# Permuted moving weights in five down-projection chunks of a hybrid decoder layer

## The chip, the cores and the metric

The kernel runs on one core of one Trainium2 chip. The metric is the device time of one execution in microseconds (us), given as the median of the runs. A profile of one execution, taken by the hardware profiler, shows what each engine did: TensorE (PE in the profile, with PEld for its weight loads), VectorE (DVE), ScalarE (ACT), GpSimd (POOL) and SyncE (SP).

## What is computed

One decoder layer on 256 tokens of width 2048, all in float32. The part around the change is the second half of the layer, the MLP, with its residual add and the last norm:

```python
x = x + mixed @ w_out[l]
h = rms_norm(x, norm2_g[l])
x = x + jnp.square(jax.nn.relu(h @ w_mlp_in[l])) @ w_mlp_out[l]
return rms_norm(x, final_norm_g)
```

`w_mlp_in` is 2048 x 8192 and `w_mlp_out` is 8192 x 2048. Ahead of it stand an input projection, a forgetting attention and a dilated attention, which the change does not touch.

## The kernel before

**Two parts for each number.** A float32 product is made of three products of a reduced type (`fp32r`): each operand is split into a high part, rounded to `fp32r`, and a low part, the rest. ACT writes the high part (`whi`) from the loaded weights (`raw`), and DVE subtracts it from the weights to get the low part (`wlo`). TensorE then adds high times high, high times low and low times high into one PSUM bank.

**Chunks and steps.** The weights are cut into chunks of 512 columns. The MLP runs in four rounds r = 0 to 3. In each round four chunks `u` (columns of `w_mlp_in`) give 2048 hidden values, and four chunks `d` (key `(r, c)`, 512 columns c of `w_mlp_out`, 2048 rows r) add them into the output. A chunk has 16 row blocks of 128, and a step is two of them, so that a plain chunk has 8 steps. `split` makes the two parts of one step's weights (128 partitions x 1024 numbers), and `products` multiplies them.

**Plain and seven.** Of the sixteen `d` chunks ten go through seven products in place of eight (`split_seven`, `seven_products`, with sub-steps "near", "first", "odd" and "even"). The other six are plain: (0,3), (1,3), (2,3), (3,0), (3,2) and (3,3). The last of them, (3,3), has code of its own (`last_chunk`). `weave` strings the steps of a plain chunk and of units of seven into one order, by patterns that are written out by hand; chunk (r,3) of the first three rounds, for example, follows `"1 A2 2 A3 2 B0"`: one plain step, then a unit of seven, and so on.

**A plain `d` step on TensorE.** `product` is called with `parts` = 2, so that each row block and each half of the tokens (128 of 256) takes two halves of 256 columns with three products each: 2 row blocks x 2 token halves x 2 column halves x 3 = 24 matmuls. The activations are the stationary operand (`big_hi`, `big_lo`), and the weights are the moving operand, 256 columns at a time, which lie in order in `whi` and `wlo`.

**The split of a plain step** is one ACT instruction and one DVE instruction over the whole step:

```python
nc.scalar.activation(hi[:, :, c:c + step], t[:, :, c:c + step], AF.Copy)
...
nc.vector.tensor_tensor(lo, t, hi.bitcast(F32), op=ALU.subtract)
```

**What sets the order.** Each engine runs its instructions in the order in which the program gives them. Splits are made some steps ahead of the products: as many as tiles are free for `whi` and `wlo` (four from one pool, and a fifth pair, `whi5` and `wlo5`, in the MLP). A split therefore waits until TensorE has finished with an older step's tile. Between the splits stand the side works, which `at` puts behind given steps: `drain_u`, `rest_u`, `mix_activations` and `split_mixed` for the hidden values, `drain_seven` and `drain_d` for the output.

Of the kernel before, what the change touches and what calls it, by code (L numbers as in the profile page):

```python
# [28 lines left out]
CW = 512  # L29
# [46 lines left out]
def kernel(  # L76
# [18 lines left out]
    nc = tc.nc  # L95
# [22 lines left out]
    def take_bank():  # L118

        n = free_banks.pop(0)  # L120
        t = psum.tile([P, CW], F32, name=f"bank{n}")
        number[id(t)] = n
        return t
# [4 lines left out]
    chunks = []  # L128
# [4 lines left out]
    for g, (vc, qc, kc, half, kind) in enumerate(groups):  # L133
        for what, c0 in (("q", qc), ("v", vc), ("k", kc)):
            cols = CW + NH if (g == 0 and what == "v") else CW
# [65 lines left out]
    raws, splits = {}, {}  # L201
# [30 lines left out]
    def drop(ci, unit):  # L232
        free_raws.append(slots.pop((ci, unit)))
# [44 lines left out]
    def split(i, j0=0, n=2):  # L278
# [13 lines left out]
        splits[i] = (hi, lo)  # L292
        split_rows(i, j0, n)

    def split_rows(i, j, n):
        ci, s, _ = steps[i]
        if s % 2 and j + n == 2:
            drop(ci, s // 2)
        hi, lo = (a[:, j:j + n, :] for a in splits[i])
        t = raws[ci, s // 2][:, 2 * (s % 2) + j:2 * (s % 2) + j + n, :chunks[ci][5]]  # L300
        cols = t.shape[2]
        step = cols // 2 if i == j == 0 else cols
        for c in range(0, cols, step):
            nc.scalar.activation(hi[:, :, c:c + step], t[:, :, c:c + step], AF.Copy)  # L304
        nc.vector.tensor_tensor(lo, t, hi.bitcast(F32), op=ALU.subtract)  # L305
# [169 lines left out]
    accs = {}  # L475

    def operands(what, key):
        if what == "o":
            return yT_hi, yT_lo, key[0] * NH
        if what == "d":  # L480
            return *squares(), 0
        return aT_hi, aT_lo, 0

    def product(acc, a, kt, t, w, j, cols, go, end, narrow=False):

        (ah, al, base), (hi, lo) = a, w
        xh, xl = (p[:, base + kt, t * P:(t + 1) * P] for p in (ah, al))
        for n, (x, part) in enumerate(((xh, hi), (xh, lo), (xl, hi)) if narrow else ((xh, hi), (xl, hi), (xh, lo))):
            nc.tensor.matmul(acc, x, part[:, j, cols], start=go and n == 0, stop=end and n == 2,  # L489
                             skip_group_check=True)  # L490

    def turned_product(ci, i, j, kt, kts):


        if kt == 0:
            accs[ci] = [take_bank() for _ in range(2)]
        hi, lo = splits[i]
        terms = ((hi, aT_hi), (hi, aT_lo), (lo, aT_hi))
        order = [(b, n) for b in range(4) for n in range(3)]
        if i == j == 0:  # L500
            order.sort(key=lambda bn: bn[1])
        for b, n in order:
            acc = accs[ci][b // 2][:, b % 2 * SEQ:(b % 2 + 1) * SEQ]
            w, a = terms[n]
            nc.tensor.matmul(acc, w[:, j, b * P:(b + 1) * P], a[:, kt, :],  # L505
                             start=kt == 0 and b % 2 == 0 and n == 0, stop=kt == kts - 1 and n == 2,
                             skip_group_check=True)

    def products(i, j):
        ci, s, sub = steps[i]  # L510
        what, key, _, _, _, cols, kts = chunks[ci]
        if sub:
            return seven_products(i, j)
        kt = 2 * s + j
        if what in TURNED:
            return turned_product(ci, i, j, kt, kts)
        a = operands(what, key)
        if ci in mixed:
            for t in range(TB):
                product(held(ci, t), a, kt, t, splits[i], j, slice(0, CW), first_in(ci, t), i == last_step[ci] and j == 1)  # L520
            return
        if cols > CW:
            return gated_products(ci, i, j, kt, kts, a)
        if kt == 0:
            accs[ci] = [take_bank() for _ in range(TB)]
        go, end = kt == 0, kt == kts - 1
        parts = 2 if what == "d" else 1
        for t in range(TB):
            for c in range(0, CW, CW // parts):
                cols = slice(c, c + CW // parts)  # L530
                product(accs[ci][t][:, cols], a, kt, t, splits[i], j, cols, go and c == 0, end, parts > 1)

    begun_banks = set()

    def held(ci, n):
        four_banks = accs.setdefault(ci, [None] * 4)
        if four_banks[n] is None:
            four_banks[n] = take_bank()
        return four_banks[n]

    def first_in(ci, n):
        fresh = (ci, n) not in begun_banks
        begun_banks.add((ci, n))
        return fresh

    def seven_products(i, j):

        ci, s, sub = steps[i]
        half, k1, k2 = CW // 2, 2 * s + j, 2 * s + 2 + j
        lower, upper = slice(0, P), slice(P, SEQ)  # L550
        if ci in mixed:
            h, m, base = (aT_hi, aT_lo), forms, KT - FIRST
        else:
            h, m, base = squares(), (mix_hi, mix_lo), 0
        todo = {
            "near": ((0, 0, h, k2, lower), (0, half, m, k2 - base, lower)),
            "first": ((2, 0, h, k1, lower),),
            "odd": ((3 if ci in mixed else 1, half, m, k2 - base, upper), (2, half, m, k1 - base, lower)),
            "even": ((3, 0, m, k1 - base, upper), (1, 0, h, k2, upper)),
        }[sub]  # L560
        hi, lo = splits[i]
        for n, (bank, c0, (ah, al), k, tokens) in enumerate(todo):
            acc = held(ci, bank)[:, c0:c0 + half]
            fresh = first_in(ci, bank)
            for x, (a, w) in enumerate(((ah, hi), (ah, lo), (al, hi))):
                nc.tensor.matmul(acc, a[:, k, tokens], w[:, j, n * half:(n + 1) * half], start=fresh and x == 0,  # L566
                                 stop=s == KT // 2 - 2 and j == 1 and x == 2, skip_group_check=True)

    def gated_products(ci, i, j, kt, kts, a):

        if kt == 0:
            accs[ci] = [take_bank() for _ in range(3)]
        half = CW // 2
        for t in range(TB):
            for acc, c0, c1, go in ((accs[ci][0][:, t * half:(t + 1) * half], 0, half, t == 0),
                                    (accs[ci][1 + t][:, :half + NH], half, CW + NH, True)):
                product(acc, a, kt, t, splits[i], j, slice(c0, c1), go and kt == 0, kt == kts - 1)
# [528 lines left out]
    for ci, (what, key, *_rest) in enumerate(chunks[:-1]):  # L1106
        e = last_slot[what, key]
# [11 lines left out]
        elif what in "qk":  # L1119
# [90 lines left out]
    for i in range(final):  # L1210
        if i == mlp_start:
            attention.close()
            late5 = ctx.enter_context(tc.tile_pool(name="late5", bufs=1))
            late5.tile([P, 24], F32R, name="late_begin")
            late = late_forms.enter_context(tc.tile_pool(name="late", bufs=1))
            late_tiles.update(ring=late5, pool=late)
            for n in ("whi5", "wlo5"):
                late5.tile([P, 2 * CW + LINE], F32R, name=n)
            late5.tile([P, 2, CW // 2], F32, name="copies")
            late5.tile([P, 4, CW], F32, name="raw4")  # L1220
            free_raws.append(4)
            late.tile([P, MIX_HI], F32R, name="late_hi")
            mix_hi = late.tile([P, KT, SEQ], F32R, name="mix_hi")
            late.tile([P, MIX_LO], F32R, name="late_lo")
            mix_lo = late.tile([P, KT, SEQ], F32R, name="mix_lo")
            late.tile([P, LINE - (MIX_HI + MIX_LO) % LINE], F32R, name="late_end")
        load_more()
        while free_tiles(i) if i + LEAD < final else done < upto.get(i, i + LEAD):
            done += 1
            split(done)  # L1230
            load_more()
        for j in range(2):
            products(i, j)
            run_side(2 * i + j)
# [31 lines left out]
```

## Time and profile before

| | |
|---|---|
| median of 2 runs | 1072.07 us (1072.02 to 1072.12) |
| profiled execution, its own time | 1072.24 us |
| its span | 1070.5 us |
| mean granted TensorE clock | 0.998 |
| PE busy | 1059.5 us, 8729 matmuls |
| DVE busy | 879.1 us, 1228 instructions |
| ACT busy | 633.4 us, 881 instructions |
| HBM read | 220.09 MB |

The span runs from the first to the last instruction that the profile shows; the execution's own time has 1.74 us more around it. The duration of a matmul in the profile is the time it spends in a pipeline, and several overlap; what one matmul costs in a stream is the distance from start to start, which the chain of work shows (a time divided by a count). For the other engines a mean duration is what an instruction occupies, with little overlap between neighbours.

### The profile page before, as it was taken

The page shows a single profiled execution, that of the slowest core. Times are in us where ns is not written, and L with a number is a line of the kernel's source. Part 1 is how long each engine was busy: PE and PEld are TensorE (multiplying, and loading weights), DVE is VectorE, ACT ScalarE, POOL GpSimd, SP SyncE. Part 2 cuts the span into 40 slices and gives each one's busy share as a digit, 9 for nine tenths or more (in the row PEclk, how much of TensorE's full clock was granted, in tenths as well). Part 3 has the DMA queues.
Part 4 walks back from the last instruction along what each step waited for, and adds up shares of the span by engine and source line. Part 5 has one row for each costly group of instructions (what it writes and reads, how often), then busy time and mean ns, then how long its engine had stood idle before and what let it go on. Part 6 is the DMA issues. An engine that isn't in the chain of part 4 may idle for free.

```text
span 1070.5 us, 21145 instructions
## 1 busy us (share of the span) xinstructions
PE 1059.5 (99%) x8729; PEld 1033.2 (97%) x8729; DVE 879.1 (82%) x1228; ACT 633.4 (59%) x881; POOL 85.2 (8%) x88
## 2 busy tenths in 40 slices
PE   9999999999999999999999999999999999999996
PEld 7999999999988889999999999999999999999996
DVE  6687797887786666678989898988898998897885
ACT  6555556556555565566556666556666656766551
POOL 0011211101001000000100001000000110000000
PEclk9999999999999999999999999999999999999999
DMA  9765565466665567657786677776768776674762
GB/s 322 244 206 189 144 230 162 137 226 179 220 243 173 169 225 216 200 165 217 220 268 173 208 246 237 226 214 196 247 184 257 221 246 215 187 273 146 215 227 80
DMA packets 118189, 223.57 MB, mean 209 GB/s; under 512 B 4723, under 2 KB 17612, under 8 KB 117708
## 3 DMA queue, kind: packets, MB, share of 16 engines
q1 hardware_dynamic: 104684, 208.69, 57.5%
q0 software_dynamic: 12816, 13.12, 8.0%
q8 instruction: 68, 1.11, 0.4%
q10 hardware_dynamic: 592, 0.40, 0.2%
q14 instruction: 29, 0.24, 0.1%
HBM read 220.09 MB, written 2.11 MB: 208 GB/s over the span
## 4 chain that ended last, share of the span: by engine, by line
PE 99%; DMA 0%; DVE 0%; POOL 0%; ACTq 0%; DVEq 0%; issue 0%
PE bank L505 49%; PE bank L489 26%; PE bank L566 21%; PE bank L428 1%; PE bank L880 1%; PE bank L820 1%; PE bank L860 0%; DMA xs<-in_x_dram 0%; PE bank L816 0%; PE bank L882 0%; PE bank L810 0%; PE bank L814 0%; DVE xs L1075 0%; PE bank L884 0%; PE bank L644 0%; POOL rstd L1065 0%
## 5 line engine op out<-in xcount | busy, mean ns | idle before, releaser
L505 PE MATMUL bank<-aT_hi,whi 128*128 128x256 f32 x1536 | 427.1, 278 | 0.0
L505 PE MATMUL bank<-aT_hi,wlo 128*128 128x256 f32 x1536 | 424.4, 277 | 0.0
L505 PE MATMUL bank<-aT_lo,whi 128*128 128x256 f32 x1536 | 424.2, 276 | 0.0
L305 DVE TENSOR_TENSOR wlo<-raw,whi 128x1024 fp32r<-128x1024 f32 (+2 forms) x291 | 349.9, 1215 | 70.7 <-ACT whi L304 68.4
L304 ACT ACTIVATE whi<-raw 128x1024 fp32r<-128x1024 f32 (+2 forms) x292 | 300.6, 1045 | 89.3 <-PE bank L505 39.2
L505 PEld LDWEIGHTS bank<-aT_hi,whi 128*128 128x128 f32 x1536 | 288.2, 188 | 1.1 <-issue 0.9
L505 PEld LDWEIGHTS bank<-aT_lo,whi 128*128 128x128 f32 x1536 | 288.4, 188 | 0.2
L505 PEld LDWEIGHTS bank<-aT_hi,wlo 128*128 128x128 f32 x1536 | 288.3, 188 | 0.1
L267 ACT ACTIVATE whi<-raw 128x1024 fp32r<-128x1024 f32 (+1 forms) x178 | 167.3, 948 | 160.4 <-PE bank L505 55.7
L268 DVE TENSOR_TENSOR wlo<-raw,whi 128x1024 fp32r<-128x1024 f32 (+1 forms) x178 | 194.6, 1095 | 52.6 <-ACT whi L267 50.7
L489 PE MATMUL bank<-whi,big_hi 128*128 128x256 f32 (+1 forms) x488 | 150.3, 308 | 0.0
L489 PE MATMUL bank<-wlo,big_hi 128*128 128x256 f32 (+1 forms) x488 | 149.4, 306 | 0.0
L489 PE MATMUL bank<-whi,big_lo 128*128 128x256 f32 (+1 forms) x488 | 149.3, 306 | 0.0
L489 PEld LDWEIGHTS bank<-wlo,big_hi 128*128 128x128 f32 x488 | 91.6, 188 | 5.1
L489 PEld LDWEIGHTS bank<-whi,big_hi 128*128 128x128 f32 x488 | 91.7, 188 | 4.5
L489 PEld LDWEIGHTS bank<-whi,big_lo 128*128 128x128 f32 x488 | 91.7, 188 | 4.5
L220 POOL DMA_DIRECT2D raw<-in_w_mlp_out_dram x40 | 48.1, 1203 | 559.3 <-DMA raw<-in_w_mlp_out_dram 252.7
L566 PE MATMUL bank<-whi,mix_lo 128*128 128x256 f32 x320 | 88.4, 276 | 0.0
L566 PE MATMUL bank<-whi,mix_hi 128*128 128x256 f32 x320 | 88.4, 276 | 0.0
L566 PE MATMUL bank<-wlo,mix_hi 128*128 128x256 f32 x320 | 88.4, 276 | 0.0
L566 PE MATMUL bank<-whi,big_hi 128*128 128x256 f32 x240 | 66.3, 276 | 0.0
L566 PE MATMUL bank<-whi,big_lo 128*128 128x256 f32 x240 | 66.3, 276 | 0.0
(228 smaller groups left out, 1436.7 us busy)
## 6 DMA issues: line engine op xcount, KB each, us to landing
raw<-in_w_mlp_in_dram SPq DMA_DIRECT2D x64, 1024.0 KB, 6.1
raw<-in_w_mlp_out_dram SPq DMA_DIRECT2D x64, 1024.0 KB, 6.7
raw<-in_w_in_dram SPq DMA_DIRECT2D x42, 1024.0 KB, 5.3
raw<-in_w_out_dram SPq DMA_DIRECT2D x16, 1024.0 KB, 5.1
raw<-in_w_mlp_out_dram POOLq DMA_DIRECT2D x40, 256.0 KB, 4.8
raw<-in_w_in_dram SPq DMA_DIRECT2D x4, 1040.0 KB, 9.6
xs<-in_x_dram SPq DMA_DIRECT2D x1, 2048.0 KB, 10.1
xs<-in_x_dram SPq DMA_DIRECT2D x3, 512.0 KB, 5.7
```

Source lines behind the costliest of these rows:

```text
L220: nc.gpsimd.dma_start(t[:, :2, CW // 2:CW], src[:, :2, :CW // 2], accum_op=ALU.add)
L267: nc.scalar.activation(hi, x, AF.Copy)
L268: nc.vector.tensor_tensor(lo, x, hi.bitcast(F32), op=ALU.subtract)
L304: nc.scalar.activation(hi[:, :, c:c + step], t[:, :, c:c + step], AF.Copy)
L305: nc.vector.tensor_tensor(lo, t, hi.bitcast(F32), op=ALU.subtract)
L428: nc.tensor.transpose(p[:, j * SEQ + t * P:j * SEQ + (t + 1) * P], xs[:, t, c:c + P], ident)
L489: nc.tensor.matmul(acc, x, part[:, j, cols], start=go and n == 0, stop=end and n == 2, skip_group_check=True)
L505: nc.tensor.matmul(acc, w[:, j, b * P:(b + 1) * P], a[:, kt, :], start=kt == 0 and b % 2 == 0 and n == 0, stop=kt == kts - 1 and n == 2, s ...
L566: nc.tensor.matmul(acc, a[:, k, tokens], w[:, j, n * half:(n + 1) * half], start=fresh and x == 0, stop=s == KT // 2 - 2 and j == 1 and x ...
L820: nc.tensor.matmul(s[:, c0:c1], q[:, a, h, rows], k[:, b, h, keys], start=False, stop=n == 2, skip_group_check=True)
L880: nc.tensor.matmul(y[:, :SEQ], v[:, 0, dims], p[:, m, :SEQ], start=n == 0, stop=False, skip_group_check=True)
```

## The change

`split_rows` gets a second way for five of the plain `d` chunks, which a table `walks` names. In this way each step is split in four pieces of 128 x 256 (two row blocks, two column halves) in place of one of 128 x 1024: four ACT and four DVE instructions. Each piece is written into its 256 places in another sequence. `written` views the loaded weights as they are, and `in_order` views the places in the order in which the columns must be read. `product` gives TensorE the view `in_order` of the moving operand, so that the columns come out in their old order. Nothing else moves: the loads, the tiles, the number of matmuls, the order of the steps and the side works stay.

The table has three numbers (a, b, e) for each chunk. The 256 places are b groups of a runs of e neighbours, and column number (i, j, k) of a x b x e lies at place (j, i, k). With e = 4, TensorE reads runs of 4 neighbours (16 bytes) and jumps between them; in places of 4 bytes:

| chunk | (a, b, e) | what TensorE reads one after the other |
|---|---|---|
| (0,3) | (32, 2, 4) | a run of 4, the run 128 places on, back to the next run |
| (1,3) | (2, 32, 4) | runs of 4, 8 places apart, in two passes |
| (2,3) | (4, 16, 4) | runs of 4, 16 places apart, in four passes |
| (3,0) | (2, 128, 1) | single numbers, 2 places apart, in two passes |
| (3,2) | (8, 8, 4) | runs of 4, 32 places apart, in eight passes |

```diff
@@ split_rows
+    walks = {(0, 3): (32, 2, 4), (1, 3): (2, 32, 4), (2, 3): (4, 16, 4), (3, 0): (2, 128, 1), (3, 2): (8, 8, 4)}
+
+    def walk(ci):
+        what, key = chunks[ci][:2]
+        return walks.get(key) if what == "d" else None
+
+    def in_order(x, ci):
+        a, b, e = walk(ci)
+        if b == 2:
+            return x.rearrange("p (b a e) -> p a b e", b=2, e=4)
+        if e == 1:
+            return x.rearrange("p (b a) -> p a b", a=a)
+        return x.rearrange("p (b a e) -> p a b e", a=a, e=e)
+
+    def written(x, ci):
+        a, b, e = walk(ci)
+        if b == 2:
+            return x.rearrange("p (a b e) -> p a b e", b=2, e=4)
+        if e == 1:
+            return x.rearrange("p (a b) -> p a b", a=a)
+        return x.rearrange("p (a b e) -> p a b e", a=a, e=e)
+
     def split_rows(i, j, n):
         ...
+        if walk(ci):
+            for k in range(n):
+                for c in range(0, CW, CW // 2):
+                    cs = slice(c, c + CW // 2)
+                    nc.scalar.activation(in_order(hi[:, k, cs], ci), written(t[:, k, cs], ci), AF.Copy)
+                    nc.vector.tensor_tensor(in_order(lo[:, k, cs], ci), written(t[:, k, cs], ci),
+                                            in_order(hi[:, k, cs], ci).bitcast(F32), op=ALU.subtract)
+            return
@@ product
-            nc.tensor.matmul(acc, x, part[:, j, cols], start=go and n == 0, stop=end and n == 2,
-                             skip_group_check=True)
+            y = part[:, j, cols]
+            nc.tensor.matmul(acc, x, in_order(y, ci) if ci is not None and walk(ci) else y, start=go and n == 0,
+                             stop=end and n == 2, skip_group_check=True)
@@ products
-                product(accs[ci][t][:, cols], a, kt, t, splits[i], j, cols, go and c == 0, end, parts > 1)
+                product(accs[ci][t][:, cols], a, kt, t, splits[i], j, cols, go and c == 0, end, parts > 1, ci)
```

The first place to look at is DVE's queue in chunk (1,3), from the split of its second plain step to that of its fourth. `wlo` is the low part that is written; `nat`, `big_lo` and `mix_lo` belong to the side works on the hidden values. DVE before:

```order
L305 TENSOR_TENSOR wlo<-raw_7422,whi 128x1024 [waits PE_49,Activation_49]
L961 TENSOR_TENSOR big_lo<-nat,big_hi 128x512
L961 TENSOR_TENSOR big_lo<-nat,big_hi 128x512 [waits Activation_49]
L268 TENSOR_TENSOR wlo<-raw_7442,whi 128x2x2x256 [waits Activation_49]
L968 TENSOR_TENSOR nat<-nat 128x2x128 [waits DVE_49]
L969 TENSOR_TENSOR nat<-nat 128x2x128 [waits DVE_49]
L971 TENSOR_TENSOR nat<-nat 128x2x128 [waits DVE_49]
L972 TENSOR_TENSOR nat<-nat 128x2x128 [waits DVE_49]
L305 TENSOR_TENSOR wlo_7794<-raw_7476,whi_7793 128x1024 [waits DMAHW1_49,Activation_49]
L305 TENSOR_TENSOR wlo<-raw_7476,whi 128x1024 [waits Activation_49]
```

The same place on DVE in the changed kernel, where the lines have moved down by the new functions:

```order
L328 TENSOR_TENSOR wlo<-raw_7470,whi 128x2x32x4 [waits PE_49,Activation_49]
L328 TENSOR_TENSOR wlo<-raw_7470,whi 128x2x32x4 [waits Activation_49] x3
L992 TENSOR_TENSOR big_lo<-nat,big_hi 128x512
L992 TENSOR_TENSOR big_lo<-nat,big_hi 128x512 [waits Activation_49]
L268 TENSOR_TENSOR wlo<-raw_7490,whi 128x2x2x256 [waits Activation_49]
L999 TENSOR_TENSOR nat<-nat 128x2x128 [waits DVE_49]
L1000 TENSOR_TENSOR nat<-nat 128x2x128 [waits DVE_49]
L1002 TENSOR_TENSOR nat<-nat 128x2x128 [waits DVE_49]
L1003 TENSOR_TENSOR nat<-nat 128x2x128 [waits DVE_49]
L328 TENSOR_TENSOR wlo_7854<-raw_7524,whi_7853 128x2x32x4 [waits DMAHW1_49,Activation_49]
L328 TENSOR_TENSOR wlo_7854<-raw_7524,whi_7853 128x2x32x4 [waits Activation_49] x3
L328 TENSOR_TENSOR wlo<-raw_7524,whi 128x2x32x4 [waits Activation_49] x4
```

No instruction has changed its place; where one stood for a step there are four, each of which waits for its own piece of the high part.

The second place is TensorE's queue at the start of that second plain step (`bank` is the PSUM bank of the sums). Before:

```order
L489 MATMUL bank_7738<-whi,big_hi 128x256 [waits Activation_49]
L489 MATMUL bank_7738<-wlo,big_hi 128x256 [waits DVE_49]
L489 MATMUL bank_7738<-whi,big_lo 128x256
L489 MATMUL bank_7738<-whi,big_hi 128x256
L489 MATMUL bank_7738<-wlo,big_hi 128x256
L489 MATMUL bank_7738<-whi,big_lo 128x256
```

And in the changed kernel:

```order
L520 MATMUL bank_7798<-whi,big_hi 128x256 [waits Activation_49]
L520 MATMUL bank_7798<-wlo,big_hi 128x256 [waits DVE_49]
L520 MATMUL bank_7798<-whi,big_lo 128x256
L520 MATMUL bank_7798<-whi,big_hi 128x256 [waits Activation_49]
L520 MATMUL bank_7798<-wlo,big_hi 128x256 [waits DVE_49]
L520 MATMUL bank_7798<-whi,big_lo 128x256
```

TensorE's matmuls stand as before, but a step no longer waits for its whole split at its first two matmuls: it waits four times, once for each piece, as it comes to it.

More of the change, by code (lines that the diff above doesn't have):

```diff
@@ L482, in operands, with product @@
         return aT_hi, aT_lo, 0
-    def product(acc, a, kt, t, w, j, cols, go, end, narrow=False):
+    def product(acc, a, kt, t, w, j, cols, go, end, narrow=False, ci=None):
         (ah, al, base), (hi, lo) = a, w
```

## The prediction

> **What bounds the kernel now.** I read the page's span and busy times first, then the chain of work that ended last, then that chain in order of time around the changed chunks.
>
> ```profile
> span 1070.5 us, 21145 instructions
> PE 1059.5 (99%) x8729; PEld 1033.2 (97%) x8729; DVE 879.1 (82%) x1228; ACT 633.4 (59%) x881; POOL 85.2 (8%) x88
> PE 99%; DMA 0%; DVE 0%; POOL 0%; ACTq 0%; DVEq 0%; issue 0%
> 655.21 2.72 PE bank L489 x24
> 674.25 2.72 PE bank L489 x24
> 678.33 5.44 PE bank L489 x48
> 360.03 10.91 PE bank L489 x48
> 657.93 3.40 PE bank L566 x30
> 139.09 3.50 PE bank L566 x30
> ```
>
> The chain is TensorE for 99% of the span: no engine and no transfer is waited for in the MLP, and its pieces follow each other without a gap. So the time is the number of matmuls times their distance, and the change can act in two ways: by the distance of the 256-column matmuls whose moving operand is read in another sequence, or by splits that become late. A plain step (L489 x24, starts in the first column, length in the second) takes 2.72 us, or 113.3 ns for a matmul of 256 columns. With 512 columns (10.91 for 48) it is 227.3 ns. The difference is 114.0 ns for 256 columns, 0.445 ns for one, with nothing fixed left over: what TensorE pays for is the stream of moving columns, which is exactly what the change rearranges.
>
> **The stream.** The change touches 5 chunks x 8 steps x 24 = 960 matmuls, which now take 960 x 113.3 ns = 108.8 us. No matmul of the trace reads its moving operand in runs of 4 or at a stride, so the price has to be bounded. At the lower end the distance stays 113.3 ns: all matmuls of 256 columns in the MLP have it (L566 and L489 alike), whatever tile they read, and no row shows less. At the upper end every second column slot is lost, so that 256 columns take what 512 take now: 113.9 ns more each, 109 us in all. Between them stands the one row in which the same shape is slower: 30 matmuls of L566 take 3.50 us in the attention part, 116.7 ns each, and 3.40 us in the MLP. There the operands lie at other offsets, so a shift between the two streams that TensorE reads is a possible cause; at that price 960 matmuls cost 3.2 us more.
>
> The nearest row on short runs is one of the other two engines; it stands among the rows of the splits, and with it the value that I take.
>
> **The splits.** Each of the 40 steps loses one instruction of 1024 numbers on ACT and on DVE and gets four of 256 on each.
>
> ```profile
> L305 DVE TENSOR_TENSOR wlo<-raw,whi 128x1024 fp32r<-128x1024 f32 x142 | 170.4, 1219 | 12.7 <-ACT whi L304 11.1
> L268 DVE TENSOR_TENSOR wlo<-raw,whi 128x512 fp32r<-128x512 f32 x38 | 26.0, 684 | 0.3 <-ACT whi L267 0.3
> L972 DVE TENSOR_TENSOR nat<-nat 128x256 f32<-128x256 f32 x13 | 5.5, 425 | 0.4
> L304 ACT ACTIVATE whi<-raw 128x1024 fp32r<-128x1024 f32 x142 | 145.9, 1051 | 21.6 <-PE bank L505 11.2 <-PE bank L566 6.6 <-PE bank L489 3.5
> L267 ACT ACTIVATE whi<-raw 128x512 fp32r<-128x512 f32 x38 | 23.9, 628 | 26.6 <-PE bank L505 15.1 <-PE bank L489 8.4 <-PE bank L566 1.5
> L1034 ACT ACTIVATE nat<-xs 128x256 f32<-128x256 f32 x1 | 0.4, 418 | 0.9 <-DVE xs L1040 0.9
> L414 ACT ACTIVATE p<-logf x1: 256/256/256, 63.7 to 63.7; 128x64 fp32r<-128x64 f32 x1
> L415 DVE TENSOR_TENSOR p<-logf,p x1: 225/225/225, 64.0 to 64.0; 128x64 fp32r<-128x64 f32 x1
> ```
>
> In the rows of the MLP the number behind the busy time is the mean of one instruction in ns.
>
> The last two rows write 64 numbers in 8 runs of 8, which stand 32 numbers apart (the split of the gates, `lf_hi[..., :NH]`), and DVE reads the high part in the same runs. By the rows above them, numbers that lie in order cost (684 - 425) / 256 = 1.01 ns each on DVE and (628 - 418) / 256 = 0.82 ns on ACT beside a fixed part, so that 64 in order would take 425 - 192 x 1.01 = 231 ns and 418 - 192 x 0.82 = 261 ns. Measured are 225 and 256 ns: runs cost these engines nothing, and I price the pieces as plain ones. For TensorE that is another engine and a longer run, but it is the nearest row to the rearranged reading, and it speaks for a distance that stays. I therefore take **0 us for the stream**, and keep both ends.
>
> A split costs 4 x 425 = 1700 ns on DVE in place of 1219, so 0.48 us more for a step and 3.85 us for a chunk; on ACT 4 x 418 = 1672 ns in place of 1051, 0.62 us a step and 5.0 us a chunk. That is 19 us of DVE and 25 us of ACT in all, and none of it counts as long as TensorE finds its pieces. What room there is stands in the busy times of the stretches in which the chunks run: the first three are (0,3), (1,3) and (2,3), the last holds (3,0) and (3,2) with the seven-product chunk woven in. The columns are the stretch, its length, and the busy time of PE, PEld, DVE, ACT and POOL.
>
> ```profile
> 488.00:524.00 36.00, 36.00 (x320) 36.00 (x319) 33.30 (x42) 23.41 (x29) 2.54 (x3) 1.00 0.72 211
> 653.00:689.00 36.00, 36.00 (x320) 36.00 (x319) 32.63 (x42) 24.05 (x30) 3.61 (x3) 1.00 0.73 221
> 819.00:855.00 36.00, 36.00 (x320) 36.00 (x320) 32.72 (x42) 23.98 (x30) 3.61 (x3) 1.00 0.73 219
> 950.00:1030.00 80.00, 80.00 (x708) 80.00 (x708) 65.02 (x77) 49.00 (x62) 4.81 (x4) 1.00 0.67 217
> 671.93 1.22 DVE L305 TENSOR_TENSOR wlo<-raw,whi 128x1024 fp32r<-128x1024 f32 x1
> 674.37 2.35 DVE L305 TENSOR_TENSOR wlo<-raw,whi 128x1024 fp32r<-128x1024 f32 x2
> ```
>
> DVE is free for 2.70, 3.37 and 3.28 us in the first three stretches, and 3.85 us are asked of each: 1.15, 0.48 and 0.57 us too much, 2.2 us together. The last stretch has 15.0 us for 7.7. ACT has 12 us in each of the first three for 5. So **DVE in chunks (0,3), (1,3), (2,3) is the only place where splits can become late**, and what stands there is how far ahead it is. The two DVE rows are the tightest: the split of the fifth plain step of (1,3) ends at 673.15 us, and TensorE starts that step at 674.25, 1.1 us later. Behind that split in DVE's queue stand the splits of the unit of seven and of the next two plain steps, so that a delay goes on to them until DVE is next free.
>
> Two things make the delay smaller than the deficit. Two splits that follow each other take 2.35 us together, 1.13 from start to start, since neighbours overlap by some 0.09 us; with the same overlap four pieces take 4 x 0.34 = 1.36 us and not 1.70, 0.23 more than before, 1.8 us a chunk, which is less than is free. And TensorE now waits for the first piece alone, 0.34 to 0.43 us behind the start of the split where it was 1.22, which gives back 0.8 us at each step's start; DVE in turn can begin behind the first piece of ACT. The splits cost TensorE between 0 and 2.2 us. I take **0.8 us**, nearer to zero, since the overlap row is of this very instruction.
>
> **The sum.** The profiled execution took 1072.24 us, a span of 1070.5 and 1.74 around it. With 0 for the stream and 0.8 for the splits it is 1073.0; the median of the runs is 0.17 us under the profiled execution, so that I forecast **1072.9 us**. Two per cent, 21.4 us, is about what a measurement of this kernel can tell from no change.
>
> **A rule of the Trainium skill.** In the rows every matmul of 256 moving columns pays for its columns alone. The Trainium skill, "Advanced Engine Details and Errata", section "SBUF Cachelines", says that SBUF has lines of 16 bytes and that one needs "at least two hits on a cacheline to absorb SRAM access latency". By that rule the four chunks with runs of 4 (four hits in each line) run at full speed, and (3,0), with two hits in a line and two passes, stands exactly at the edge; no run so far shows a line's worth. It would leave the sum at 1072.9, or, if two hits are not enough, give the second rival.
>
> **Rivals.**
> - *A column slot is lost at each jump.* A matmul of 256 columns in runs of 4 has 64 jumps; at 0.445 ns for a column 28.5 ns more, 192 matmuls a chunk, four chunks: 21.9 us, **1094.8, slower**. If single numbers at a stride count as jumps too, (3,0) pays 256 x 0.445 = 114 ns x 192 = 21.9 us beside it, 1116.7. It decides from a mean of 21.4 us / 960 = 22.3 ns more for a matmul. For it: the cost of a matmul is all in the columns, so that any stumble of the stream shows in full, and TensorE has no idle time to hide it. Against it: the short runs that cost DVE and ACT nothing.
> - *Only the chunk with a stride of two is slow*: its 192 matmuls take as long as with 512 columns, 192 x 113.9 ns = 21.9 us, again 1094.8. For it: it alone reads single numbers. The row of runs of 8 speaks against it, but holds no such stride.
> - *The two streams shift against each other*, as between the MLP and the attention part: 960 x 3.3 ns = 3.2 us, 1076.1. The same size with the other sign, if another sequence fits better, gives 1069.7. For the first: tiles here lie at chosen offsets, and 116.7 ns is seen. For the second no row speaks, since none is under 113.3 ns.
> - *DVE becomes the bound*, if pieces that are written in runs cost what 512 numbers cost now, 684 ns: 4 x 0.684 - 1.219 = 1.52 us a step, 12.1 a chunk. Less what is free that is 9.4 + 8.8 + 8.9 us in the first three stretches, and 24.3 - 15.0 = 9.3 in the last: 36 us, 1109. It passes 2% from 0.59 us a piece. The rows of ACT and DVE in runs of 8 speak against it.
> - *The change doesn't do what it says*: if views were merged so that TensorE reads in order after all, only the splits are left, 1072.9. The pieces' shapes in DVE's queue (128x2x32x4) speak against it.
>
> TensorE's own rule gives a little room below. The Trainium skill, "TensorE: Matmul & The Clock Gate", section "Back-to-back issue gap", has N / 2.4 + 2.5 ns for an isolated matmul, 109.2 ns for 256 columns as an estimate, where this trace has 113.3; if the rest were lost to the old sequence, up to 3.9 us could come back, 1069.
>
> **How the numbers follow.** The forecast, stream unchanged and splits hidden, 0.56 (1071.5 to 1075). A shift between the streams, slower 0.10, faster 0.05. A slot for each jump 0.13, and the stride of two alone 0.07, both with a third of their chance at smaller prices that stay within 2%. DVE as the bound 0.06. Not what it says 0.03. So: slower by over 2% about 0.13 for the jumps and the stride, and 0.06 for DVE, 0.19; faster by over 2% 0.01, for which no row speaks; within 2% 0.80. The range goes from 1069, which takes in the shift that helps, to 1096, which takes in the jumps in four chunks and the stride alone; left out are all five chunks together and DVE as the bound, some 0.13.
>
> **What would show it.** In the changed kernel's chain the plain `d` steps (L520) stand with 2.72 us for 24 matmuls in each of the five chunks. If it is the jumps, four chunks show some 3.4 us and the chunk with the stride differs; if it is the stride, only the steps of (3,0) in the last 120 us do. DVE's pieces stand at 425 ns and ACT's at 418 ns, with DVE at 35 to 36 busy of 36 us in the first three stretches. If splits are late, TensorE has idle time before L520 or before the units of seven behind it, named with DVE's `wlo`; I expect under 1 us a chunk. I would be wrong by much if TensorE's reading is priced by the jump, since there is no slack on it anywhere.

## The result and the profile after

The changed kernel takes **1102.03 us** (median of 2 runs, 1101.62 to 1102.45) where the kernel before takes 1072.07: a ratio of 1.028 with a 95% interval of 1.0235 to 1.0324. It is slower, by 30 us.

The page of the changed kernel, its first lines and its chain:

```profile
span 1099.8 us, 21385 instructions
PE 1088.4 (99%) x8729; PEld 1058.2 (96%) x8729; DVE 887.6 (81%) x1348; ACT 645.2 (59%) x1001; POOL 85.8 (8%) x88
PE 99%; DMA 0%; DVE 0%; POOL 0%; ACTq 0%; DVEq 0%; issue 0%
```

The span is 29.3 us longer, and still 99% of it is TensorE. The number of matmuls is the old one, and no engine is waited for in the MLP. So the same matmuls have become longer, and not by the clock: its granted mean is 0.997, and 0.998 before. The chain in order of time (start, length, line, count) shows which; the five steps are of (0,3), (1,3), (2,3), (3,0) and (3,2) in this order, each of 24 matmuls, where every one took 2.72 us before. The last two rows are groups of seven-product matmuls that stand behind such steps and took 3.40 us.

```profile
496.21 3.04 PE bank L520 x24
664.66 2.82 PE bank L520 x24
831.54 2.74 PE bank L520 x24
996.73 5.51 PE bank L520 x24
1042.46 2.96 PE bank L520 x24
492.78 3.43 PE bank L597 x30
854.29 3.46 PE bank L597 x30
```

| chunk | what is read one after the other | us a step | ns a matmul | more in the chunk, us |
|---|---|---|---|---|
| (0,3) | runs of 4, 128 places to and fro | 3.04 | 126.7 | 2.6 |
| (1,3) | runs of 4, 8 places apart | 2.82 | 117.6 | 0.8 |
| (2,3) | runs of 4, 16 places apart | 2.75 | 114.4 | 0.2 |
| (3,0) | single numbers, 2 places apart | 5.51 | 229.4 | 22.3 |
| (3,2) | runs of 4, 32 places apart | 2.96 | 123.2 | 1.9 |

The plain steps make 27.8 us of the 29.3. The groups behind them, at 0.02 to 0.06 us each, make 1.1 more, although neither their operands nor their own order of reading changed. The stride of two alone is 22.3 us. The splits, the other half of the change, cost what plain pieces cost (the rows give the mean of one instruction in ns behind the busy time):

```profile
L328 DVE TENSOR_TENSOR wlo<-raw,whi 128x256 fp32r<-128x256 f32 x160 | 56.2, 419 | 5.5 <-ACT whi L327 5.5
L327 ACT ACTIVATE whi<-raw 128x256 fp32r<-128x256 f32 x160 | 52.7, 408 | 13.0 <-PE bank L520 9.8 <-PE bank L536 2.1 <-PE bank L597 1.1
```

### The profile page after: what moved, and what is told of

The parts are those of the page before. It is cut to its first block, busy times and chain, and to the rows that moved or that the text cites. A ratio compares the mean times of both kernels' runs of the same rounds, so it can differ in the third digit from the quotient of the medians.

```text
span 1099.8 us, 21385 instructions
## 1 busy us (share of the span) xinstructions
PE 1088.4 (99%) x8729; PEld 1058.2 (96%) x8729; DVE 887.6 (81%) x1348; ACT 645.2 (59%) x1001; POOL 85.8 (8%) x88
## 4 chain that ended last, share of the span: by engine, by line
PE 99%; DMA 0%; DVE 0%; POOL 0%; ACTq 0%; DVEq 0%; issue 0%
PE bank L536 48%; PE bank L520 28%; PE bank L597 20%; PE bank L458 1%; PE bank L911 1%; PE bank L851 1%; PE bank L891 0%; DMA xs<-in_x_dram 0%; PE bank L847 0%; PE bank L913 0%; PE bank L841 0%; PE bank L845 0%; DVE xs L1106 0%; PE bank L915 0%; PE bank L675 0%; POOL rstd L1096 0%
## 5 line engine op out<-in xcount | busy, mean ns | idle before, releaser
L335 DVE TENSOR_TENSOR wlo<-raw,whi 128x1024 fp32r<-128x1024 f32 (+2 forms) x251 | 302.0, 1214 | 64.0 <-ACT whi L334 62.5
L334 ACT ACTIVATE whi<-raw 128x1024 fp32r<-128x1024 f32 (+3 forms) x252 | 259.5, 1045 | 83.6 <-PE bank L536 37.5
L520 PE MATMUL bank<-whi,big_hi 128*128 128x256 f32 (+1 forms) x488 | 161.3, 330 | 0.0
L520 PE MATMUL bank<-wlo,big_hi 128*128 128x256 f32 (+1 forms) x488 | 160.7, 329 | 0.0
L520 PE MATMUL bank<-whi,big_lo 128*128 128x256 f32 (+1 forms) x488 | 160.5, 329 | 0.0
```

What stands on the lines that cost most here:

```text
L520: nc.tensor.matmul(acc, x, in_order(y, ci) if ci is not None and walk(ci) else y, start=go and n == 0, stop=end and n == 2, skip_group_che ...
```

## The experiments

The theory at this point was that all of it is TensorE's own reading (A). Its rivals were that the pieces that ACT and DVE write out of order disturb TensorE (B), and that more instructions make splits late (C).

### The reading alone (e1)

The splits are those of the kernel before; the views of TensorE stay. In the changed kernel's code:

```diff
-        if walk(ci):
+        if False:
             for k in range(n):
```

> The splits are those of the kernel before (one ACT and one DVE instruction of 1024 numbers a step, written in order); only TensorE reads the five chunks in the five sequences, so that the columns of these chunks come out permuted. Theory A (the cost lies in TensorE's own reading): a plain step takes what it takes in the changed kernel, 3.04 us in (0,3), 2.82 in (1,3), 2.75 in (2,3), 5.51 in (3,0), 2.96 in (3,2), and the time is 1099 to 1102 us. Rival B (the pieces of ACT and DVE, written in runs or at a stride, disturb TensorE's streams): the steps take 2.72 us and the time is 1072 us. If both act, (3,0) stays near 5.5 us and the units of seven beside the chunks fall back from 3.43 to 3.46 us to 3.40.

Measured: 1102.16 us, ratio 1.0267 (1.0252 to 1.0282), as slow as the whole change. The chain has a step of (0,3) and one of (3,0) at the very lengths of the changed kernel; the other three chunks agree too (2.82, 2.75, 2.96), and so do the groups behind them:

```profile
495.92 3.04 PE bank L520 x24
996.44 5.51 PE bank L520 x24
492.49 3.43 PE bank L597 x30
```

### The writing alone (e2), and plain pieces (e3)

e2 keeps the four pieces in their five sequences, and lets TensorE read in order. e3 keeps four pieces, but writes and reads in order.

```diff
-            nc.tensor.matmul(acc, x, in_order(y, ci) if ci is not None and walk(ci) else y, start=go and n == 0,
+            nc.tensor.matmul(acc, x, y, start=go and n == 0,
```

> The splits are those of the changed kernel (four pieces, written in the five sequences), but TensorE reads the places in order, so that the weights of the five chunks are multiplied in a permuted order of columns. Theory A: all plain steps take 2.72 us, 1072 to 1073 us. Rival B: the steps keep 2.75 to 5.51 us, 1099 to 1102 us. If only the small costs come from the writing: (3,0) at 2.72 us, the units of seven at 3.43 to 3.46 us in place of 3.40, and 1073 to 1077 us.

> Four pieces a step as in the changed kernel, but written and read in order. Theory A and rival B both expect 2.72 us for every plain step and 1072 to 1073 us. Rival C (more instructions on ACT and DVE make splits late): idle time on TensorE before plain steps or units of seven, 1073 to 1075 us.

Measured: e2 1073.45 us, ratio 1.0001 (0.9991 to 1.0010); e3 1074.35 us, ratio 1.0007 (0.9996 to 1.0017), both beside a median of 1073.78 for the kernel before in those runs. Steps of (0,3) and (3,0) in e2, then a step of (0,3) and the two u steps right behind (1,3) in e3:

```profile
497.20 2.72 PE bank L520 x24
1001.43 2.72 PE bank L520 x24
...
508.24 2.72 PE bank L519 x24
691.25 5.64 PE bank L535 x48
```

Rival B falls: pieces written in any of the five sequences leave TensorE alone. Rival C is right in kind and very small: the two u steps behind (1,3) take 5.64 us in place of 5.44, and those behind (0,3) and (2,3) 5.53, as splits come late there by 0.1 to 0.2 us; e3's span is 1070.8 us, 0.3 more than before. The changed kernel does not show even this: its u steps behind the three chunks take 5.44 us.

### The sequences dealt anew (e4), and without the stride (e12)

```diff
-    walks = {(0, 3): (32, 2, 4), (1, 3): (2, 32, 4), (2, 3): (4, 16, 4), (3, 0): (2, 128, 1), (3, 2): (8, 8, 4)}
+    walks = {(0, 3): (2, 128, 1), (1, 3): (4, 16, 4), (2, 3): (8, 8, 4), (3, 0): (32, 2, 4), (3, 2): (2, 32, 4)}
```

> The changed kernel with the same five sequences dealt to other chunks: (0,3) has the stride of two, (1,3) runs 16 places apart, (2,3) runs 32 places apart, (3,0) runs 128 places apart, (3,2) runs 8 places apart. If the cost belongs to the sequence: 5.5, 2.75, 2.96, 3.04 and 2.82 us a step. If it belongs to the place in the program (round 3 has more DMA or other neighbours): (3,0) stays at 5.5 us. Time 1099 to 1103 us either way.

Measured: 1102.19 us. The cost went with the sequence to its new chunk; here are steps of (0,3) and of (3,0):

```profile
500.24 5.51 PE bank L516 x24
1014.25 3.04 PE bank L516 x24
```

In e12 the changed kernel lost only the entry `(3, 0): (2, 128, 1)` of the table.

> The changed kernel with chunk (3,0) left as it was before; the other four chunks keep their sequences. If the stride of two is the main cost, 8 steps x (5.51 - 2.72) us and the groups beside them go: 1102 - 22.6 = 1079.4 us, and the rest stays as 0.32, 0.10, 0.03 and 0.24 us a step in the four chunks and the groups behind them. If a slow chunk hides something of the others' costs or makes splits early, 1075 or 1083 us.

Measured: 1078.97 us, ratio 1.0058 (1.0044 to 1.0072), 23.1 us less than the changed kernel. The steps of (3,0) are back at 2.72 us, and the other four chunks kept their lengths. The costs add up: the stride's 22.3 us are gone, and those of the other sequences stay.

### What TensorE's reading pays for (e5, e8, e9)

These probes leave the splits as before and change only the view of the moving operand in the five chunks, so that columns come out permuted there; e8 shifts the start of the tiles too. Each ran once, and its u steps, which stay at 2.72 us, are the yardstick in its own trace. In e5, in the changed kernel's code (the views also lose their special case for b = 2, which fixed e at 4):

```diff
-    walks = {(0, 3): (32, 2, 4), (1, 3): (2, 32, 4), (2, 3): (4, 16, 4), (3, 0): (2, 128, 1), (3, 2): (8, 8, 4)}
+    walks = {(0, 3): (2, 64, 2), (1, 3): (64, 2, 2), (2, 3): (8, 32, 1), (3, 0): (128, 2, 1), (3, 2): (4, 64, 1)}
 ...
-        if walk(ci):
+        if False:
```

> Only TensorE's reading is changed (plain splits; columns come out permuted). Sequences: (0,3) pairs 4 places apart, (1,3) pairs alternating 128 places, (2,3) single numbers 8 places apart, (3,0) single numbers alternating 128 places, (3,2) single numbers 4 places apart. Theory F8 (TensorE takes the moving operand 8 bytes, two numbers, at a time): the pairs stay at 2.7 to 3.4 us a step, all singles take 5.5 us; three chunks at double, 1072 + 67 + up to 12 = 1139 to 1151 us. Theory F16 (it takes lines of 16 bytes, four numbers): pairs take 5.5 us like the stride of two, which also uses two numbers of four, and singles with a line each take 10.9 us; 1072 + 2 x 22 + 3 x 66 = 1314 us. Theory S (any innermost step other than one halves the rate): as F8 here; the run with straddling pairs tells these two apart.

> Only TensorE's reading and the offsets in the tiles are changed: (0,3) in order from the odd place 9, (1,3) pairs 4 places apart from the odd place 9, (2,3) runs of 4, 16 places apart, from place 10, so that each crosses a 16-byte boundary, (3,0) in order from place 24, (3,2) runs of 4, 16 places apart, from place 24. F8: straddling pairs 5.5 us, runs of 4 from place 10 stay near 2.75, order from an odd place near 2.72. F16: straddling pairs take at least 5.5 and runs across a boundary 5.5. S: straddling pairs as fast as aligned ones. The chunks in order from 24 take 2.72, or other than 2.72 if the offset against the stationary operand matters.

> Only TensorE's reading is changed. Theory D: TensorE takes the columns two at a time, the even and the odd ones by separate ways, and each way needs two successive numbers out of one 16-byte line to keep pace; otherwise it takes twice the time. Rival L: what counts is how often a line has to be fetched for four columns, with recently used lines kept at hand. With places of a 256-block numbered 0 to 255: (0,3) 0, 128, 2, 130, 4, ... then the odd places the same way (each way sees two numbers of a line, each line is visited in two passes): D 2.7 us a step, L 5.5. (1,3) 0, 64, 128, 192, 1, 65, ... (each way changes its line every time, four lines at hand): D 4.0 to 5.5, L 2.7. (2,3) 0, 4, 1, 5, 2, 6, 3, 7, 8, 12, ...: both 2.7. (3,0) 0, 64, 1, 65, ... within halves of 128: both 2.7. (3,2) 0, 128, 4, 132, ... in four passes (each way has one number of a line): both 5.5.

| run, chunk | places read one after the other | us a step | ns a matmul |
|---|---|---|---|
| before | 0, 1, 2, 3, ... | 2.72 | 113.3 |
| e5 (0,3) | pairs: 0, 1, 4, 5, 8, ... | 5.51 | 229.6 |
| e5 (1,3) | pairs: 0, 1, 128, 129, 2, 3, ... | 4.05 | 168.7 |
| e5 (2,3) | 0, 8, 16, ... | 5.23 | 217.9 |
| e5 (3,0) | 0, 128, 1, 129, 2, ... | 2.68 | 111.7 |
| e5 (3,2) | 0, 4, 8, ... | 5.59 | 232.9 |
| e8 (0,3) | in order, from the odd place 9 | 2.92 | 121.7 |
| e8 (1,3) | pairs 4 apart, from 9 | 5.52 | 230.0 |
| e8 (2,3) | runs of 4, 16 apart, from 10 (each crosses a 16-byte boundary) | 5.54 | 230.8 |
| e8 (3,0) | in order, from 24 | 2.85 | 118.8 |
| e8 (3,2) | runs of 4, 16 apart, from 24 | 2.73 | 113.8 |
| e9 (0,3) | 0, 128, 2, 130, 4, ... | 2.72 | 113.3 |
| e9 (1,3) | 0, 64, 128, 192, 1, 65, ... | 3.36 | 140.0 |
| e9 (2,3) | 0, 4, 1, 5, 2, 6, 3, 7, 8, ... | 2.68 | 111.7 |
| e9 (3,0) | 0, 64, 1, 65, ... | 2.68 | 111.7 |
| e9 (3,2) | 0, 128, 4, 132, ... | 5.51 | 229.6 |

The chain of e5 for pairs, for singles 128 places to and fro, and for singles 4 apart; that of e8 for the runs of 4 from place 10, for the order from place 24 and for the runs of 4 from place 24; and that of e9 for its first, second, third and fifth chunk:

```profile
499.97 5.51 PE bank L516 x24
1041.97 2.68 PE bank L516 x24
1073.36 5.59 PE bank L516 x24
...
847.21 5.54 PE bank L518 x24
1035.48 2.85 PE bank L518 x24
1065.01 2.73 PE bank L518 x24
...
497.17 2.72 PE bank L512 x24
663.78 3.36 PE bank L512 x24
834.39 2.68 PE bank L512 x24
1024.60 5.51 PE bank L512 x24
```

All three theories of e5 had a miss. The whole run took 1150.92 us, inside F8's 1139 to 1151, but by luck: its slow chunks are in part others than F8 had named. Pairs are slow, against F8 and S. Singles with a line each take twice and not four times the time, against F16. And singles 128 places to and fro are not slow at all, against all three; they are *faster* than reading in order. The runs across a 16-byte boundary (e8) show that the line counts: the same runs of 4 take 5.54 us from place 10, and 2.73 to 2.75 us from 8 or 24.

Theory D, made from this, says that even and odd columns are read by separate ways, and that each way keeps pace if two successive numbers of its own come out of one 16-byte line. In order, each way has two of a line (113.3 ns). At a stride of two, in pairs 4 apart, or in runs that straddle a boundary each has one: 229 to 231 ns. Singles 4 and 8 places apart have one too, at 232.9 and 217.9 ns. In 0, 128, 1, 129 each has four: 111.7. Forecast ahead of e9 were 2.7 us for 0, 128, 2, 130 in two passes, which uses as few numbers of each line in a pass as the slow stride of two, 2.7 for 0, 4, 1, 5 and 5.5 for 0, 128, 4, 132: measured are 2.72, 2.68 and 5.51. Rival L, by which each fetch of a line has to serve four columns, had 5.5 for the first.

The two ways themselves are seen in no trace; D is a rule that was drawn from e5 and e8 and held in these three readings of e9. It is not the whole of it. With four places 64 apart each way changes its line at every column, and D expected 4.0 to 5.5 us; measured are 3.36. The alternating pairs, 4.05 us, are also less than double. A line that was left a moment ago may come cheaper; no run tried that. Nor does D say anything of the small costs of the runs of 4, where each way has its two of a line.

### The small costs (e6, e7, e10)

Only the views and, in e7 and e10, the start of the five chunks' tiles differ:

```diff
+            if what == "d":
+                high = low = {(0, 3): 0, (1, 3): 24, (2, 3): 40, (3, 0): 24, (3, 2): 24}.get(chunks[ci][1], NEAR)
```

> Only TensorE's reading is changed. Sequences: (0,3) runs of 4, 64 places apart in groups of 4, (1,3) runs of 8 alternating 128 places, (2,3) runs of 8, 16 places apart, (3,0) runs of 16 alternating 128 places, (3,2) runs of 8, 32 places apart. Theory J (a price for each jump, set by its distance): the extra of a step halves from runs of 4 to runs of 8 and again to runs of 16: from 0.32 us for 128 places to 0.16 and 0.08, from 0.24 for 32 places to 0.12; 64 places between 0.24 and 0.32. Theory P (the sequence meets the stream of the stationary operand, whose address runs on in order): no simple halving, since the meeting depends on how the address moves over a whole matmul. Time 1074 to 1078 us.

> Only TensorE's reading is changed, and the five chunks' weights begin at other offsets in their tiles (in places; 8 before): runs of 4 alternating 128 places at offset 0 in (0,3), 24 in (1,3) and 40 in (2,3); runs 8 places apart at 24 in (3,0); runs 32 places apart at 24 in (3,2). Theory J (a price for each jump): 3.04, 3.04, 3.04, 2.82 and 2.96 us a step as at offset 8; 1078 us. Theory P (it meets the stationary operand's stream): the three equal sequences differ from each other by tenths of a us, and one of them may come near 2.72.

> Only TensorE's reading and the offsets are changed: all five chunks are read as 0, 128, 1, 129, 2, ..., which took 2.68 us a step at offset 8, with their weights at offsets 0, 16, 24, 40 and 56 in (0,3), (1,3), (2,3), (3,0) and (3,2). Theory D alone: 2.68 us in all five, 1070 to 1072 us. If the offset against the stationary operand's stream decides the rest, as for reading in order (2.72 us from 8, 2.85 from 24): the five differ by up to 0.15 us, and one may be under 2.68.

e6 in its five chunks, e7 in its first three, and e10 in its first and fourth, with a group behind the first; then a group behind the first chunk of e9, and one behind the fourth of e8, which reads in order from place 24:

```profile
498.07 3.29 PE bank L516 x24
668.45 2.95 PE bank L516 x24
836.45 2.83 PE bank L516 x24
996.89 2.88 PE bank L516 x24
1026.66 2.81 PE bank L516 x24
...
497.89 3.09 PE bank L518 x24
667.03 3.10 PE bank L518 x24
836.11 3.06 PE bank L518 x24
...
495.29 2.68 PE bank L514 x24
985.90 2.68 PE bank L514 x24
491.84 3.45 PE bank L591 x30
...
493.77 3.40 PE bank L589 x30
...
1045.42 3.47 PE bank L595 x30
```

Theory J (a fixed price for each jump) fails: 128 places to and fro cost 0.32 us a step in runs of 4, 0.23 in runs of 8 and 0.16 in runs of 16, not half each time, and runs that jump 16 places take 2.83 us in eights and 2.75 in fours. Runs of 4 that jump 64 places are dearer (3.29) than those that jump 128 (3.04), so the distance alone does not set it either. The whole runs took 1084.95 us (e6) and 1086.48 (e7), above their forecasts (1074 to 1078, and 1078).

Of theory P only this is seen, that the start of the tile matters: a little for runs (3.04 to 3.10 us, not tenths, and none came near 2.72), more for reading in order, which takes 2.72 us from place 8 and 2.85 from 24. That the meeting with the stationary operand does it is not shown. For the steps that read 0, 128, 1, 129 the start makes no difference, at 2.68 us from five starts, all multiples of 8.

What sets the small costs, 5.5 us of the 29, stays open, and so does what sets the 0.02 to 0.06 us of the groups behind. In e10 they are mostly 0.05 us where the chunk starts at 0, 24 or 56 and 0.02 at 16 or 40, some 1.0 us in all of the 1.6 that the 40 steps gain. Behind the sequence 0, 128, 2, 130 of e9 there is nothing (3.40 us), and behind steps in order from 24 there are up to 0.07 (3.47 us in e8). So it is neither a price of every rearranged reading nor only of rearranged ones.

### Versions that use the faster reading (e11, e13, e14)

If all MLP matmuls of 256 columns are read as 0, 128, 1, 129, ..., 1.6 ns on each of some 5900 is worth 9.5 us. Three versions differ in who puts the order of the `d` chunks right. In the `u` chunks the moving operand is the activations, and in all three versions ACT and DVE bring these into place as they split them out of PSUM. e11 writes the weights at the places where they must lie:

```diff
+    def split_down(i, flat, x):
+        hi, lo = (a.rearrange("p (g b a) -> p g a b", b=2, a=CW // 4) for a in flat)
+        x = x.rearrange("p g (a b) -> p g a b", b=2)
+        nc.scalar.activation(hi, x, AF.Copy)
+        nc.vector.tensor_tensor(lo, x, hi.bitcast(F32), op=ALU.subtract)
```

> A version built from the runs: the moving operand of all MLP products of 256 columns (the plain and seven-product d chunks and the u chunks) is read as 0, 128, 1, 129, ..., and written so that the columns come out in order; one ACT and one DVE instruction a split as in the kernel before. The steps of 24 should go from 2.72 to 2.68 us, the groups of 30 from 3.40 to 3.35; some 5900 matmuls times 1.6 ns, 9.5 us less than before: 1062 to 1064 us. If the cost at the change between two kinds of reading (3.45 for 3.40 us behind such a step) comes with each group and not with the change of kind, the gain is less: 1068 to 1071 us. If splits written at a distance are dearer for ACT and DVE than in the changed kernel's pieces (412 to 429 ns on DVE), TensorE waits and it is slower than 1072 us.

Measured: 1247.94 us, ratio 1.1638 (1.1622 to 1.1654). The splits take twice as long, and TensorE waits for splits, 115 us in all by the list of waits (the third row below is its first: us in total, times, longest). The granted clock is also lower in this run, 0.970 in the mean where the kernel before has 0.998, and in stretches behind long waits matmuls stand 0.21 us apart in place of 0.11.

```profile
L263 ACT ACTIVATE whi<-raw 128x1024 fp32r<-128x1024 f32 x165 | 347.4, 2215 | 165.5 <-DVE raw L290 77.2 <-PE bank L592 47.9 <-DVE raw L293 27.3
L264 DVE TENSOR_TENSOR wlo<-raw,whi 128x1024 fp32r<-128x1024 f32 x165 | 351.0, 2155 | 73.4 <-ACT whi L263 73.4
PE bank L592 <- DVE wlo L264: 46.9, 49, 1.9
```

e13 goes through the places in order and takes the loaded weights at a stride of two:

```diff
-        hi, lo = (a.rearrange("p (g b a) -> p g a b", b=2, a=CW // 4) for a in flat)
-        x = x.rearrange("p g (a b) -> p g a b", b=2)
+        hi, lo = (a.rearrange("p (g b a) -> p g b a", b=2, a=CW // 4) for a in flat)
+        x = x.rearrange("p g (a b) -> p g b a", b=2)
```

> As the version before it, but ACT and DVE go through the places in order and take the loaded weights at a stride of two, in place of writing single numbers 128 places apart. If the doubled splits (2.2 us for 1024 numbers on ACT and on DVE in place of 1.06 and 1.22) came from the writing at 128 places, they go back to 1.05 to 1.25 us, TensorE waits no more and takes 2.68 us for a step of 24 and 3.35 for a group of 30: 1062 to 1064 us. If single numbers out of order cost ACT and DVE double on the reading side too, it stays near 1240 us. If the price of 0.05 us behind each such step comes with every group, 1068 to 1071 us.

Measured: 1082.58 us, ratio 1.0086 (1.0072 to 1.0100). The doubling is gone, but not all of the price: 1388 ns on ACT and 1346 on DVE, where 1055 and 1222 are paid for 1024 numbers in order. That is enough to make splits late again; the list of waits has 9.6 us for them, and the rest of the 20 us above the forecast was not followed.

```profile
L263 ACT ACTIVATE whi<-raw 128x1024 fp32r<-128x1024 f32 x165 | 225.0, 1388 | 120.0 <-DVE raw L290 65.1 <-DVE raw L293 41.9 <-PE bank L531 9.8
L264 DVE TENSOR_TENSOR wlo<-raw,whi 128x1024 fp32r<-128x1024 f32 x165 | 220.7, 1346 | 53.9 <-ACT whi L263 53.6
```

e14 leaves weights and their splits as they were in the kernel before. The sums of the `d` chunks come out as 0, 128, 1, 129, ..., and DVE puts them right as it adds them into the output:

```diff
+    def add_in_order(x, acc, scale):
+        for c in range(0, x.shape[1], CW // 2):
+            xc = x[:, c:c + CW // 2].rearrange("p (b a) -> p b a", b=2)
+            part = acc[:, c:c + CW // 2].rearrange("p (a b) -> p b a", b=2)
+            nc.vector.scalar_tensor_tensor(xc, part, scale, xc, op0=ALU.mult, op1=ALU.add)
 ...
-            nc.tensor.matmul(acc, x, part[:, j, cols], start=go and n == 0, stop=end and n == 2,
+            y = part[:, j, cols]
+            nc.tensor.matmul(acc, x, alternate(y) if narrow else y, start=go and n == 0, stop=end and n == 2,
```

> The same reading (0, 128, 1, 129, ...) of the moving operand in all MLP products of 256 columns, but the splits are those of the kernel before: the weights lie in order, and the order of the sums is put right where DVE adds them into the output, which reads PSUM at a stride of two in pieces of 256 (some 50 more DVE instructions of 0.2 us net). If the splits' price was all that stood against the gain, TensorE waits nowhere in the MLP, takes 2.68 us for a step of 24 and 3.35 for a group of 30, and the time is 1062 to 1064 us. If the reading of PSUM at a stride is dear for DVE, splits behind the drains are late: 1066 to 1080 us.

Measured: **1064.19 us**, ratio 0.9912 (0.9897 to 0.9926) to the kernel before: faster, by less than 2% but clear of 1. Its span, a group of 30, a step of 24, a split in (3,2) and the step that waits for it, and the additions into the output, with those of 256 sums in the kernel before as the last row:

```profile
span 1062.9 us, 21186 instructions
491.17 3.35 PE bank L580 x30
494.51 2.68 PE bank L502 x24
1006.59 1.24 DVE wlo L314
1007.87 2.83 PE bank L502 x23
L262 DVE SCALAR_TENSOR_TENSOR xs<-bank,rstd2sq,xs 128x256 f32<-128x256 f32 x114 | 49.7, 477 | 3.6 <-PE bank L502 2.8
...
L1005 DVE SCALAR_TENSOR_TENSOR xs<-bank,rstd2sq,xs 128x256 f32<-128x256 f32 x30 | 13.5, 478 | 0.4
```

Every step and group of the MLP but that one has 111.7 ns a matmul, and no group pays more behind a step. DVE pays 477 ns for 256 sums at a stride of two in PSUM, where 478 was the price in order. Additions of 512 (746 ns) became two of 256, so that DVE has 41 more instructions. The span is 7.6 us shorter and not 9.5: the MLP begins 0.6 us later, and the step shown ends 1.6 us late.

## Why the prediction was wrong

**What bounds the kernel** was read rightly: TensorE has no idle time, so that anything its stream pays shows in full.

**The stream: 0 us.** This is the step that failed: the term of the sum for TensorE's reading was put at nothing, and it measured 27.8 us on the steps and 1.1 on the groups behind them. Of these, 22.3 us are the stride of two, where a matmul takes 229.4 ns in place of 113.3. The bounds held (0 to 109 us), but the value between them came from ACT and DVE, whose runs of 8 cost nothing. e1 and e2 show why that row could not carry it: the same sequences that cost ACT and DVE nothing to write cost TensorE 29 us to read. And e11 shows that the row did not even speak for ACT and DVE in general, since singles 128 places apart double both.

**The stride of two**, the second rival with a chance of 0.07, has the right place and price, 22.3 us against the 21.9 worked out, but named no mechanism. I had set the rule of the Trainium skill ("Advanced Engine Details and Errata", section "SBUF Cachelines", at least two hits on a line) beside it and let the chunk stand "at the edge". Two hits in a line were not enough here; the measurement decides. If hits are counted for even and odd columns apart (theory D), the count fits the readings that take double, with the two misses told above and the small costs left open.

**A slot at each jump**, the first rival, had the sign but not the mechanism: it asked for 28.5 ns a matmul, and the runs of 4 cost 1.1 to 13.4 ns with the same 64 jumps, so it is not the count of jumps that sets it.

**The shift between the streams** had about the size of the small costs, 3.2 us against the 5.5 of the four chunks. That reading depends on where a tile begins is seen in e7 and e8, but not that it explains them.

**The range** ended at 1096 since it took in either the stride or smaller costs, and not both: 1072.1 + 22.3 + 6.6 is 1101.

**The splits: 0.8 us.** The term was small, as forecast: e3's span has 0.3 more, and in the changed kernel TensorE waits for no piece. The three chunks were right, but the delay of e3 stands at the u steps behind them, and not at the steps or units of seven that I had named. Pieces at 419 and 408 ns were forecast at 425 and 418. The 35 to 36 busy us of 36 for DVE did not come: it was busy for 31.9 and 32.6 us in 36 us of (0,3) and of (1,3), and four pieces in a row take 1.43 us, near the 1.36 of the estimate with overlap.

## What to carry to other kernels

Where TensorE is the bound, the order in which it reads its moving operand can be a price on every matmul, and what other engines paid for the same pattern here said nothing about it: probe it with the writes left alone. Columns of 4 bytes at a stride of two took twice the time, and so did pairs 4 places apart and runs that straddle 16 bytes. Of the three places tried for a reordering, the additions of the sums were the one that paid: the stride cost nothing there, and in the splits of the weights it cost more than it gained.

## What the runs showed that was not expected

- Two sequences interleaved column by column (0, 128, 1, 129, ...; also 64 or 4 places apart) are read faster than one in order, 111.7 against 113.3 ns for 256 columns. For those 128 apart the five starts that were tried made no difference.
- ACT and DVE have their own such prices: writing single numbers 128 places to and fro (on DVE also reading the high part so) took 2215 and 2155 ns for 1024 in place of 1055 and 1222, while a stride of two in the writes cost nothing (408 and 419 ns a piece of 256 over all five sequences).
- How a step reads can cost the group of matmuls behind it, whose own reading is in order, up to 0.07 us; which readings do so was not found.
